# A key's cumulative gate row read from DRAM instead of multiplied out by a selector, and narrow gate weights loaded in an earlier stage

## The chip, the cores and the metric

The kernel runs on one core of one Trainium2 chip. The metric is the device time of one execution in microseconds (us), lower is better. One execution of the program was also recorded by the hardware profiler; rows below come from that record. The engines are named as in the profile: PE is TensorE (matmul), PEld its weight loads, DVE is VectorE, ACT is ScalarE, POOL is GpSimd and SP is SyncE, which here only issues DMAs.

## The reference

The program computes two layers of a decoder on 256 tokens of width 2048. Layer 0 mixes tokens by gated linear attention, layer 1 by "forgetting attention" (FoX, 16 heads of 128); each mixer is followed by a gated MLP with a short convolution (inner width 5632). All is modulated by a conditioning vector `c` through `w_mod`. The change touches the FoX mixer:

```python
def fox_mixer(h, w_in, b_f, q_gain, k_gain, w_out):
    proj = h @ w_in
    q, k, v, og, fl = jnp.split(proj, [D_MODEL, 2 * D_MODEL, 3 * D_MODEL, 4 * D_MODEL], axis=-1)
    ...
    log_f = jax.nn.log_sigmoid((fl + b_f).astype(jnp.float32))
    cum = jnp.cumsum(log_f, axis=1).transpose(0, 2, 1)
    ...
        logits = (jnp.einsum('bhqd,bhkd->bhqk', qb, k).astype(jnp.float32)
                  + cb[..., None] - cum[:, :, None, :])
        logits = jnp.where(key_pos[None, :] <= q_pos[:, None], logits, -jnp.inf)
        p = jax.nn.softmax(logits, axis=-1)
```

`fl` has one column per head (16 columns at the end of `w_in`, the "gate weights"). `cum` is the running sum of the log gates over the tokens. A logit of query i and key j gets `cum[i]` added, which is one number per query, and `cum[j]` subtracted, which is one number per key.

## The kernel before

**Streams.** All large products run in the same way. A weight tile of 128 x 1024 (512 KB) is loaded by SP into a ring of eight buffers (`sync_load`, L259 to L264; `load_to`, L727). ACT casts it into a high part `wh` (L140) and DVE subtracts to get the low part `wl` (L144), both in `split_w`. A product takes three matmuls: high by high, high by low, low by high. `plan` lists all weight tiles in the order of use. `next_w` (L699) hands out the tile of one step, splits up to three steps ahead (`AHEAD`; there are four pairs of split buffers), and loads six further (`LOOK`). Loads of the modulation weights `wm` share the ring and SP's queue.

**Steps.** One step k takes one weight tile against one slice of 128 inputs. `stream_a` (matmul at L779, 24 of 256 columns per step) puts tokens on the free side; `stream_b` (matmul at L860, 12 of 512 columns per step) puts tokens on the partitions. After each step `tick` runs small tasks from the list `side` (as many as `pace["side"]`, about one per step) and background sums of the modulation weights on DVE (L291).

**Order.** The kernel's text gives a program order, and a scheduler that simulates times puts each engine's instructions in a fixed order. Each engine then runs its own list strictly in that order, and waits on semaphores. `issue_after` asks the scheduler to place one instruction behind another. SP's list holds the DMA issues, which stop when the next buffer of the ring isn't free.

**The entry to FoX.** `fox` (L1189) first streams V in two halves of 16 steps. With the first half goes the gate projection, `gate_part`, called once a step as `extra`. From step `GATE_AT` = 9 on, it runs three matmuls a step (L1231) with the gate weights, thirty of them at step 9 for the steps before. The gate weights are one entry of the plan, placed behind step 9's tile: 2048 rows of 16 numbers (64 bytes a row), 128 KB in all, through SP and a ring buffer, split like the others into a tile `nw` of 128 x 368. Then come the log sigmoid and, as a side task, `cums`: transposes to token order (`ltok`), running sums through a triangular matrix `tri`, once per token (`cumt`, the query's number) and once as rows by head (`pn`). The rows are negated and split into a high part (partitions 0 to 15) and a low part (32 to 47) of `nhl`.

**The attention.** Q and K are streamed in four groups; behind each pair `attend(g)` puts the tasks of eight heads on `side`. For head i these are `soft` (scores and softmax), two heads later `turn` (transposes of the weights), three heads later `apply` (product with V). So the first heads of a group follow each other by one or two tasks, later ones by three. In `soft`, the key's row comes onto the scores by a matmul: `sel`, one column of `identr` repeated over 128 columns, picks the two rows of the head out of `nhl` and writes their sum to all 128 partitions in PSUM (L1292, 48 rows by 384 columns), and the score matmuls (L1293, L1294) add to it. DVE adds the query's number while it copies PSUM to the tile `s` (L1296, L1298), POOL masks it (L1301), DVE and ACT form the softmax (L1304 to L1312). There are four buffers for `s` (`SB`).

**Queues.** Loads of weights go through SP. ACT's own queue takes a few small loads at the start and half of the output at the end.

Of the kernel before, what the change touches and what calls it, by code (L numbers as in the profile page):

```python
# [9 lines left out]
F32 = mybir.dt.float32  # L10
# [59 lines left out]
NBIG = 12  # L70
FILL = (0, 7)
FIRST_ORDER = (0, 2, 1)
GATE_AT = 9
TURNS = (0, 2, 1, 3, 4, 6, 5, 7)

HELD = (16, 48)
# [4 lines left out]
def kernel(  # L81
# [46 lines left out]

    def split_w(src, moving, after=None):
        n_ = src.shape[-1]  # L130
        if n_ < 512 and not moving and n_ > 256:
            st = big.tile([P, 2, 512], F32R, tag="s8", name=nm("nw"))
            hi, lo = st[:, 0, :n_], st[:, 1, :n_]
        else:
            hi, lo = split_pair(n_, moving)
        with ExitStack() as es:
            if order["f"] is not None:
                es.enter_context(tc.issue_after(order["f"]))
                order["f"] = None
            order["b"], order["c"] = order["c"], nc.scalar.copy(out=hi, in_=src).ins  # L140
        with ExitStack() as es:
            if after is not None:
                es.enter_context(tc.issue_after(after))
            order["v"] = nc.vector.tensor_tensor(out=lo, in0=src, in1=hi.bitcast(F32), op=ALU.subtract).ins  # L144
        return hi, lo
# [5 lines left out]
    ident = const.tile([P, P], F32, name="ident")  # L151
    make_identity(nc, ident)

    H2 = 2 * FH + 16
    identr = const.tile([H2, FH], F32R, name="identr")
    nc.vector.tensor_tensor(out=identr, in0=ident[:H2, :FH], in1=ident[:H2, 32:32 + FH], op=ALU.add)
    ones = const.tile([P, P], F32, name="ones")
    nc.vector.memset(ones, 1.0)
    one = ones[:, 0:1]
# [1026 lines left out]
        add_residual(l, "g_m", ALL, rhs)  # L1186


    def fox(l, h):  # L1189
# [3 lines left out]
        nhl = tmp.tile([H2, 3 * P], F32R, tag="k1", bufs=1, name="nhl")  # L1193
        ltok = tmp.tile([P, 2, H2], F32, tag="ltok", bufs=1, name="ltok")

        def cums():
            pl = misc()
            for tt in range(TT):
                nc.tensor.transpose(pl[:, tt * FH:(tt + 1) * FH], lf[:, tt * P:(tt + 1) * P], ident[:FH, :FH])
            nc.vector.memset(ltok, 0.0)  # L1200
            for c0 in (0, 32):
                nc.vector.tensor_copy(out=ltok[:, :, c0:c0 + FH], in_=pl[:, :2 * FH].rearrange("p (a b) -> p a b", a=2))
            pc = misc()
            nc.tensor.matmul(pc[:, 0:FH], tri, ltok[:, 0, :FH], start=True, stop=True)
            nc.tensor.matmul(pc[:, FH:2 * FH], ones, ltok[:, 0, :FH], start=True, stop=False)
            nc.tensor.matmul(pc[:, FH:2 * FH], tri, ltok[:, 1, :FH], start=False, stop=True)
            nc.vector.tensor_copy(out=cumt, in_=pc[:, :2 * FH].rearrange("p (a b) -> p a b", a=2))
            pn = misc()
            nc.tensor.matmul(pn[:H2, 0:P], ltok[:, 0, :], tri, start=True, stop=True)
            nc.tensor.matmul(pn[:H2, P:T], ltok[:, 0, :], ones, start=True, stop=False)  # L1210
            nc.tensor.matmul(pn[:H2, P:T], ltok[:, 1, :], tri, start=False, stop=True)
            for cs, src in ((slice(0, P), pn[:H2, 0:P]), (slice(P, 3 * P), pn[:H2, 0:T])):
                nc.scalar.activation(nhl[:, cs], src, AF.Copy, scale=-1.0)
                lo = nhl[32:H2, cs]
                nc.vector.scalar_tensor_tensor(out=lo, in0=src[32:H2], scalar=-1.0, in1=lo.bitcast(F32),
                                               op0=ALU.mult, op1=ALU.subtract)

        pace["side"], pace["sacc"] = 1.0, 0.0
        vt = [bigt([P, D], "v") for _ in range(TT)]
        gates = {}  # L1220

        def gate_part(k):
            if k < GATE_AT:
                return
            if k == GATE_AT:
                gates["w"], gates["p"] = next_w(0, [(4 * D, FH)]), misc()
            for kk in range(0 if k == GATE_AT else k, k + 1):
                gh, gl = h(kk)
                cs = slice(kk * FH, kk * FH + P)
                for i, (w_, r_) in enumerate(((gates["w"][0], gh), (gates["w"][0], gl), (gates["w"][1], gh))):  # L1230
                    nc.tensor.matmul(gates["p"][:, :T], w_[:, cs], r_, start=(kk == 0 and i == 0),  # L1231
                                     stop=(kk == KT - 1 and i == 2), skip_group_check=True)
# [49 lines left out]
                side.append(fin(hp))  # L1282

        pts = {}

        def soft(hd):
            def f():
                q_ = qT[hd // 8][:, hd % 8, :]
                k_ = kT[hd // 8][:, hd % 8, :]
                sel = identr[:, hd:hd + 1].to_broadcast([H2, P])  # L1290
                p_ = misc()
                nc.tensor.matmul(p_[:, 0:3 * P], sel, nhl, start=True, stop=False, skip_group_check=True)  # L1292
                nc.tensor.matmul(p_[:, 0:P], q_[:, 0:P], k_[:, 0:P], start=False, stop=False, skip_group_check=True)  # L1293
                nc.tensor.matmul(p_[:, P:3 * P], q_[:, P:T], k_, start=False, stop=True, skip_group_check=True)  # L1294
# [3 lines left out]
                nc.vector.tensor_scalar(out=s[:, P:3 * P], in0=p_[:, P:3 * P], scalar1=cumt[:, 1, hd:hd + 1],  # L1298
                                        scalar2=None, op0=ALU.add)
# [301 lines left out]
    def between():  # L1601
# [1 line left out]
        queue(mod_tasks(0, "g_f"))  # L1603
        queue_halves(1, "m")
        pace["bg"] = SLOW
    ffn(0, lazy(make_h(0, "f"), KT, 2, (8,)), (ALL[:8], between, lambda: set_pace(N2)))
    drain_bg()

    queue(mod_tasks(1, "g_m"))
# [59 lines left out]
```

## Time and profile before

| | us |
|---|---|
| median of three runs | 2412.05 |
| lowest and highest of the three | 2410.41 and 2412.06 |
| the profiled execution, its own time | 2411.13 |
| its span, first to last instruction | 2409.4 |

| engine | busy us | share of the span |
|---|---|---|
| PE | 2369.6 | 98% |
| PEld | 2274.7 | 94% |
| DVE | 1886.2 | 78% |
| ACT | 1347.1 | 56% |
| POOL | 45.6 | 2% |

The mean granted clock of PE was 0.996. DMA moved 638.31 MB, a mean of 265 GB/s.

How to read it: the span is cut by engine, and engines run side by side, so busy times add up to more than the span. A matmul's busy time reaches from its start to its last result, and the next one starts before that; the distance of two starts tells what a matmul costs in a full stream. "Idle before" is the time an engine stood ahead of an instruction, with what ended it. The chain of waits follows the path back from the last instruction.

### The profile page before, as it was taken

The numbers are of one execution on the slowest core, as the hardware profiler recorded it, in microseconds if no ns is written. First come the engines' busy times: TensorE is split into PE (matmuls) and PEld (weight loads), VectorE is DVE, ScalarE is ACT, GpSimd is POOL, SyncE is SP. The second block draws the span as 40 slices with busy tenths as digits, with TensorE's granted clock in tenths as the row PEclk, the third lists the DMA queues.
The fourth block names the chain that finished last, engine by engine and source line by source line (L and its number), as shares of the span: only waits on it lengthen the run. The fifth ranks groups of instructions, "written<-read, shape, count | busy, mean of one in ns | idle before, by whom it ended". The sixth has DMA issues, their size and how long they took to land.

```text
span 2409.4 us, 46946 instructions
## 1 busy us (share of the span) xinstructions
PE 2369.6 (98%) x19028; PEld 2274.7 (94%) x19030; DVE 1886.2 (78%) x2478; ACT 1347.1 (56%) x1932; POOL 45.6 (2%) x93
## 2 busy tenths in 40 slices
PE   7999999999999999999999999999999999999998
PEld 5899889999999999999888879999999999999998
DVE  5787979887679999986678888888777777777544
ACT  4668764645776566443554455545755555565433
POOL 0000000000000000000000201100000000000000
PEclk9999999999999999999999999999999999999999
DMA  9898869797669988998589877786777777766552
GB/s 375 326 353 297 312 229 325 275 361 273 199 200 310 314 310 311 324 315 301 158 297 314 303 267 236 241 296 234 227 236 237 228 235 236 235 206 216 192 191 101
DMA packets 188293, 638.31 MB, mean 265 GB/s; under 512 B 23849, under 2 KB 24859, under 8 KB 187692
## 3 DMA queue, kind: packets, MB, share of 16 engines
q1 hardware_dynamic: 187112, 634.12, 77.0%
q8 instruction: 149, 2.44, 0.4%
q10 hardware_dynamic: 964, 1.20, 0.1%
q14 instruction: 68, 0.56, 0.1%
HBM read 633.14 MB, written 2.10 MB: 264 GB/s over the span
## 4 chain that ended last, share of the span: by engine, by line
PE 92%; DVE 3%; DMA 3%; ACT 1%; issue 1%; DVEq 0%; SPq 0%; ACTq 0%
PE pa L779 74%; PE pa L860 14%; DMA wm<-in_w_mod_dram 1%; DVE wl L144 1%; DMA w<-in_fox_w_in_dram 0%; DVE acc L291 0%; DMA w<-in_gla_w_in_dram 0%; DVE hn L623 0%; PE pm L1103 0%; PE pm L1330 0%; PE pm L1276 0%; PE pm L1294 0%; ACT wh L140 0%; PE pm L1293 0%; PE pm L1125 0%
## 5 line engine op out<-in xcount | busy, mean ns | idle before, releaser
L140 ACT CAST wh<-w 128x1024 fp32r<-128x1024 f32 x816 | 852.1, 1049 | 903.2 <-PE pa L779 651.4
L144 DVE TENSOR_TENSOR wl<-w,wh 128x1024 fp32r<-128x1024 f32 x816 | 991.7, 1218 | 405.4 <-ACT wh L140 399.3
L779 PE MATMUL pa<-h,wh 128*128 128x256 f32 x7168 | 1223.5, 278 | 5.0 <-DVE h L653 3.6
L779 PEld LDWEIGHTS pa<-h,wh 128*128 128x128 f32 x7168 | 1073.9, 188 | 10.5 <-DVE h L653 4.2
L779 PE MATMUL pa<-h,wl 128*128 128x256 f32 x3584 | 966.3, 277 | 1.9 <-DVE wl L144 1.9
L779 PEld LDWEIGHTS pa<-h,wl 128*128 128x128 f32 x3584 | 662.5, 188 | 2.7 <-DVE wl L144 2.5
L779 PE MATMUL pa<-op,wh 128*128 128x256 f32 x3840 | 651.6, 277 | 0.4 <-DVE op L683 0.2
L779 PEld LDWEIGHTS pa<-op,wh 128*128 128x128 f32 x3840 | 573.0, 188 | 1.4 <-DVE xT L912 1.0
L779 PE MATMUL pa<-op,wl 128*128 128x256 f32 x1920 | 518.0, 276 | 0.0
L291 DVE SCALAR_TENSOR_TENSOR acc<-wm,cT,acc 128x1024 f32<-128x1024 f32 (+2 forms) x360 | 444.4, 1235 | 15.1 <-DMA wm<-in_w_mod_dram 13.9
L779 PEld LDWEIGHTS pa<-op,wl 128*128 128x128 f32 x1920 | 355.0, 188 | 0.0
L860 PE MATMUL pa<-wh,h 128*128 128x512 f32 x1024 | 312.0, 394 | 0.2 <-ACT h L644 0.2
L860 PEld LDWEIGHTS pa<-wh,h 128*128 128x128 f32 x1024 | 191.1, 188 | 40.3 <-ACT h L644 0.9
L860 PE MATMUL pa<-wl,h 128*128 128x512 f32 x512 | 191.8, 394 | 0.0
L860 PEld LDWEIGHTS pa<-wl,h 128*128 128x128 f32 x512 | 96.5, 189 | 19.5
L1382 ACT ACTIVATE y<-u,cw 128x256 f32<-128x256 f32 x176 | 101.7, 599 | 3.3 <-DVE act L1398 1.3
L1385 DVE SCALAR_TENSOR_TENSOR y<-u,cw,y 128x254 f32<-128x254 f32 x176 | 83.3, 479 | 2.9
L1383 DVE SCALAR_TENSOR_TENSOR y<-u,cw,y 128x255 f32<-128x255 f32 x176 | 84.0, 477 | 0.0
L1404 ACT COPY u<-pa 128x512 f32<-128x512 f32 x112 | 63.6, 582 | 2.1 <-PE pa L779 1.2
L644 ACT ACTIVATE h<-hn,mod 128x256 fp32r<-128x256 f32 x58 | 32.4, 596 | 14.0 <-DVE hn L623 11.3
L1392 ACT ACTIVATE u<-y 128x256 f32<-128x256 f32 x88 | 36.0, 413 | 3.3 <-DVE y L1385 3.1
L1398 DVE TENSOR_TENSOR act<-u,y 128x256 f32<-128x256 f32 x88 | 36.7, 420 | 1.4
(274 smaller groups left out, 1044.5 us busy)
## 6 DMA issues: line engine op xcount, KB each, us to landing
wm<-in_w_mod_dram SPq DMA_DIRECT2D x320, 512.0 KB, 5.3
w<-in_ffn_w_up_dram SPq DMA_DIRECT2D x320, 512.0 KB, 4.5
w<-in_ffn_w_down_dram SPq DMA_DIRECT2D x176, 512.0 KB, 4.6
w<-in_fox_w_in_dram SPq DMA_DIRECT2D x128, 512.0 KB, 5.2
w<-in_gla_w_in_dram SPq DMA_DIRECT2D x96, 512.0 KB, 7.1
w<-in_gla_w_out_dram SPq DMA_DIRECT2D x32, 512.0 KB, 5.9
w<-in_ffn_w_up_dram SPq DMA_DIRECT2D x64, 256.0 KB, 4.0
w<-in_fox_w_out_dram SPq DMA_DIRECT2D x32, 512.0 KB, 5.1
```

Of the source, the lines that this page charges most:

```text
L140: order["b"], order["c"] = order["c"], nc.scalar.copy(out=hi, in_=src).ins
L144: order["v"] = nc.vector.tensor_tensor(out=lo, in0=src, in1=hi.bitcast(F32), op=ALU.subtract).ins
L291: nc.vector.scalar_tensor_tensor(out=st["a"], in0=wt[:, j, :], scalar=col, in1=st["a"], op0=ALU.mult, op1=ALU.add)
L644: hot = nc.scalar.activation(hi, t, AF.Identity, scale=sc, bias=sh).ins
L779: mm = nc.tensor.matmul(o, w_[:, ms], r_, start=(first and i == 0 and m % 2 == 0), stop=last and i == 2, skip_group_check=True)
L860: mm = nc.tensor.matmul(o, l_[:, ts_], w_[:, hs_], start=first and i == 0, stop=last and i == 2, skip_group_check=True)
L1382: nc.scalar.activation(y, u, AF.Identity, scale=cw[:, l * 3 + 2, r:r + 1], bias=cw[:, 6 + l, r:r + 1])
L1383: nc.vector.scalar_tensor_tensor(out=y[:, 1:], in0=u[:, :T - 1], scalar=cw[:, l * 3 + 1, r:r + 1], in1=y[:, 1:], op0=ALU.mult, op1=ALU.add)
L1385: nc.vector.scalar_tensor_tensor(out=y[:, 2:], in0=u[:, :T - 2], scalar=cw[:, l * 3, r:r + 1], in1=y[:, 2:], op0=ALU.mult, op1=ALU.add)
L1392: nc.scalar.activation(u, y, AF.Silu)
L1398: nc.vector.tensor_tensor(out=act[m // 8][:, m % 8, :], in0=sg, in1=y, op=ALU.mult)
L1404: nc.scalar.copy(out=u[:, 2 * b:2 * b + 2, :], in_=ps[b])
```

## The change

**The gate weights.** They leave the plan. A new function `load_gate` clears the tail of a tile of 128 x 368 on POOL and loads the 128 KB from ACT's queue. It is called from `settle`, which the first MLP runs at the start of the seventh of its up-projection's column groups. `gate_part` now makes the cast (ACT) and the subtraction (DVE) itself at step `GATE_AT` - 2 = 5 of the first V half, placed behind the last weight cast and subtraction issued by then. The gate matmuls start at step 7 (24 at once, then three a step).

**The key's row.** `nhl`, `identr` and the selector matmul go. `cums` copies the rows `pn` to SBUF on ACT and stores them with SP into a DRAM tensor `crows` of 16 x 256. `key_row(hd)` takes a buffer of `s` and loads row `hd`, repeated over 128 partitions, into its columns 128 to 383, through SP. It is called at the start of `soft` for the next head, and for the first head of a group as a side task of its own. In `soft` the first score matmul starts the sum, and the two DVE instructions become `scalar_tensor_tensor`: score plus the query's number minus the row, the second of them in place.

**Beside it.** `ltok` is 16 columns per token block and not 48 and needs no clearing. A small unused tile `spare` is set to zero at the start. The branch of `split_w` for the gate weights goes.

```diff
-GATE_AT = 9
+GATE_AT = 7
...
+    dram = ctx.enter_context(tc.tile_pool(name="dram", bufs=1, space=bass.MemoryType.DRAM))
...
-    identr = const.tile([H2, FH], F32R, name="identr")
-    nc.vector.tensor_tensor(out=identr, in0=ident[:H2, :FH], in1=ident[:H2, 32:32 + FH], op=ALU.add)
+    spare = const.tile([48, FH], F32, name="spare")
+    nc.vector.memset(spare, 0.0)
...
+    def load_gate():
+        raw_gate["w"] = w_ = tmp.tile([P, GW], F32, tag="k1", bufs=1, name="rg")
+        nc.gpsimd.memset(w_[:, KT * FH:], 0.0)
+        nc.scalar.dma_start(out=w_[:, :KT * FH].rearrange("p (k r) -> p k r", r=FH),
+                            in_=fox_w_in[0, :, 4 * D:4 * D + FH].rearrange("(k p) r -> p k r", p=P))
...
-            nc.vector.memset(ltok, 0.0)
-            for c0 in (0, 32):
-                nc.vector.tensor_copy(out=ltok[:, :, c0:c0 + FH], in_=pl[:, :2 * FH].rearrange("p (a b) -> p a b", a=2))
+            nc.vector.tensor_copy(out=ltok, in_=pl[:, :2 * FH].rearrange("p (a b) -> p a b", a=2))
...
-            for cs, src in ((slice(0, P), pn[:H2, 0:P]), (slice(P, 3 * P), pn[:H2, 0:T])):
-                nc.scalar.activation(nhl[:, cs], src, AF.Copy, scale=-1.0)
-                lo = nhl[32:H2, cs]
-                nc.vector.scalar_tensor_tensor(out=lo, in0=src[32:H2], scalar=-1.0, in1=lo.bitcast(F32),
-                                               op0=ALU.mult, op1=ALU.subtract)
+            crow_ = t1("cr")[:FH, :]
+            nc.scalar.copy(out=crow_, in_=pn[:FH, :T])
+            nc.sync.dma_start(out=crows, in_=crow_)
...
         def gate_part(k):
+            if k == GATE_AT - 2:
+                with ExitStack() as es:
+                    es.enter_context(tc.issue_after(order["c"]))
+                    es.enter_context(tc.issue_after(order["v"]))
+                    st = big.tile([P, 2, 512], F32R, tag="s8", name=nm("nw"))
+                    gates["w"] = st[:, 0, :GW], st[:, 1, :GW]
+                    nc.scalar.copy(out=gates["w"][0], in_=raw_gate["w"])
+                    nc.vector.tensor_tensor(out=gates["w"][1], in0=raw_gate["w"], in1=gates["w"][0].bitcast(F32),
+                                            op=ALU.subtract)
             if k < GATE_AT:
                 return
             if k == GATE_AT:
-                gates["w"], gates["p"] = next_w(0, [(4 * D, FH)]), misc()
+                gates["p"] = misc()
...
+        def key_row(hd):
+            s = rows_of[hd] = tmp.tile([P, 3 * P], F32, tag="s", bufs=SB, name=nm("s"))
+            nc.sync.dma_start(out=s[:, P:3 * P], in_=crows[hd:hd + 1, :].to_broadcast([P, T]))
 
         def soft(hd):
             def f():
+                if hd % 8 < 7:
+                    key_row(hd + 1)
...
-                sel = identr[:, hd:hd + 1].to_broadcast([H2, P])
                 p_ = misc()
-                nc.tensor.matmul(p_[:, 0:3 * P], sel, nhl, start=True, stop=False, skip_group_check=True)
-                nc.tensor.matmul(p_[:, 0:P], q_[:, 0:P], k_[:, 0:P], start=False, stop=False, skip_group_check=True)
+                nc.tensor.matmul(p_[:, 0:P], q_[:, 0:P], k_[:, 0:P], start=True, stop=True, skip_group_check=True)
                 nc.tensor.matmul(p_[:, P:3 * P], q_[:, P:T], k_, start=False, stop=True, skip_group_check=True)
-                s = tmp.tile([P, 3 * P], F32, tag="s", bufs=SB, name=nm("s"))
-                nc.vector.tensor_scalar(out=s[:, 0:P], in0=p_[:, 0:P], scalar1=cumt[:, 0, hd:hd + 1],
-                                        scalar2=None, op0=ALU.add)
-                nc.vector.tensor_scalar(out=s[:, P:3 * P], in0=p_[:, P:3 * P], scalar1=cumt[:, 1, hd:hd + 1],
-                                        scalar2=None, op0=ALU.add)
+                s = rows_of.pop(hd)
+                nc.vector.scalar_tensor_tensor(out=s[:, 0:P], in0=p_[:, 0:P], scalar=cumt[:, 0, hd:hd + 1],
+                                               in1=s[:, P:2 * P], op0=ALU.add, op1=ALU.subtract)
+                nc.vector.scalar_tensor_tensor(out=s[:, P:3 * P], in0=p_[:, P:3 * P], scalar=cumt[:, 1, hd:hd + 1],
+                                               in1=s[:, P:3 * P], op0=ALU.add, op1=ALU.subtract)
...
         def attend(g):
             h0 = g * 8
+            side.append(lambda: key_row(h0))
...
-    plan_stream(fox_w_in[0], ALL[:GATE_AT + 1], [(2 * D, 1024)], True)
-    plan.append((fox_w_in[0], 0, KT, ((4 * D, FH),), False))
-    plan_stream(fox_w_in[0], ALL[GATE_AT + 1:], [(2 * D, 1024)], True)
-    for c0 in (2 * D + 1024, 0, D, 1024, D + 1024, 3 * D, 3 * D + 1024):
+    for c0 in (2 * D, 2 * D + 1024, 0, D, 1024, D + 1024, 3 * D, 3 * D + 1024):
         plan_stream(fox_w_in[0], ALL, [(c0, 1024)], c0 < 3 * D)
...
+    def settle():
+        set_pace(N2)
+        load_gate()
+    ffn(0, lazy(make_h(0, "f"), KT, 2, (8,)), (ALL[:8], between, settle))
```

More of the change, by code (lines that the diff above doesn't have):

```diff
@@ L130, in split_w @@
         n_ = src.shape[-1]
[L131 to L135, printed above, removed]
+        hi, lo = split_pair(n_, moving)
         with ExitStack() as es:
@@ L1186, in gla_rest @@
         add_residual(l, "g_m", ALL, rhs)
+    GW = KT * FH + P - FH
+    raw_gate = {}
+    def load_gate():
[3 more added lines that the diff above has]
+                            in_=fox_w_in[0, :, 4 * D:4 * D + FH].rearrange("(k p) r -> p k r", p=P))
     def fox(l, h):
@@ L1192, in fox @@
         cumt = tmp.tile([P, 2, FH], F32, tag="cumt", bufs=1, name="cumt")
-        nhl = tmp.tile([H2, 3 * P], F32R, tag="k1", bufs=1, name="nhl")
-        ltok = tmp.tile([P, 2, H2], F32, tag="ltok", bufs=1, name="ltok")
+        ltok = tmp.tile([P, 2, 48], F32, tag="ltok", bufs=1, name="ltok")[:, :, :FH]
+        crows = dram.tile([FH, T], F32, name="crows")
         def cums():
@@ L1199, in cums @@
                 nc.tensor.transpose(pl[:, tt * FH:(tt + 1) * FH], lf[:, tt * P:(tt + 1) * P], ident[:FH, :FH])
-            nc.vector.memset(ltok, 0.0)
-            for c0 in (0, 32):
-                nc.vector.tensor_copy(out=ltok[:, :, c0:c0 + FH], in_=pl[:, :2 * FH].rearrange("p (a b) -> p a b", a=2))
+            nc.vector.tensor_copy(out=ltok, in_=pl[:, :2 * FH].rearrange("p (a b) -> p a b", a=2))
             pc = misc()
-            nc.tensor.matmul(pc[:, 0:FH], tri, ltok[:, 0, :FH], start=True, stop=True)
-            nc.tensor.matmul(pc[:, FH:2 * FH], ones, ltok[:, 0, :FH], start=True, stop=False)
-            nc.tensor.matmul(pc[:, FH:2 * FH], tri, ltok[:, 1, :FH], start=False, stop=True)
+            nc.tensor.matmul(pc[:, 0:FH], tri, ltok[:, 0, :], start=True, stop=True)
+            nc.tensor.matmul(pc[:, FH:2 * FH], ones, ltok[:, 0, :], start=True, stop=False)
+            nc.tensor.matmul(pc[:, FH:2 * FH], tri, ltok[:, 1, :], start=False, stop=True)
             nc.vector.tensor_copy(out=cumt, in_=pc[:, :2 * FH].rearrange("p (a b) -> p a b", a=2))
             pn = misc()
-            nc.tensor.matmul(pn[:H2, 0:P], ltok[:, 0, :], tri, start=True, stop=True)
-            nc.tensor.matmul(pn[:H2, P:T], ltok[:, 0, :], ones, start=True, stop=False)
-            nc.tensor.matmul(pn[:H2, P:T], ltok[:, 1, :], tri, start=False, stop=True)
-            for cs, src in ((slice(0, P), pn[:H2, 0:P]), (slice(P, 3 * P), pn[:H2, 0:T])):
-                nc.scalar.activation(nhl[:, cs], src, AF.Copy, scale=-1.0)
-                lo = nhl[32:H2, cs]
-                nc.vector.scalar_tensor_tensor(out=lo, in0=src[32:H2], scalar=-1.0, in1=lo.bitcast(F32),
-                                               op0=ALU.mult, op1=ALU.subtract)
+            nc.tensor.matmul(pn[:FH, 0:P], ltok[:, 0, :], tri, start=True, stop=True)
+            nc.tensor.matmul(pn[:FH, P:T], ltok[:, 0, :], ones, start=True, stop=False)
+            nc.tensor.matmul(pn[:FH, P:T], ltok[:, 1, :], tri, start=False, stop=True)
+            crow_ = t1("cr")[:FH, :]
+            nc.scalar.copy(out=crow_, in_=pn[:FH, :T])
+            nc.sync.dma_start(out=crows, in_=crow_)
         pace["side"], pace["sacc"] = 1.0, 0.0
@@ L1284, in fox @@
         pts = {}
+        rows_of = {}
+        def key_row(hd):
+            s = rows_of[hd] = tmp.tile([P, 3 * P], F32, tag="s", bufs=SB, name=nm("s"))
+            nc.sync.dma_start(out=s[:, P:3 * P], in_=crows[hd:hd + 1, :].to_broadcast([P, T]))
         def soft(hd):
             def f():
+                if hd % 8 < 7:
+                    key_row(hd + 1)
                 q_ = qT[hd // 8][:, hd % 8, :]
                 k_ = kT[hd // 8][:, hd % 8, :]
[L1290 removed]
                 p_ = misc()
[L1292 to L1293 removed]
+                nc.tensor.matmul(p_[:, 0:P], q_[:, 0:P], k_[:, 0:P], start=True, stop=True, skip_group_check=True)
                 nc.tensor.matmul(p_[:, P:3 * P], q_[:, P:T], k_, start=False, stop=True, skip_group_check=True)
[L1295 to L1299 removed]
+                s = rows_of.pop(hd)
[3 more added lines that the diff above has]
+                                               in1=s[:, P:3 * P], op0=ALU.add, op1=ALU.subtract)
                 dv = s.rearrange("p (j t) -> p j t", j=3)[:, 0:3:2, :]
@@ L1605, in between @@
         pace["bg"] = SLOW
-    ffn(0, lazy(make_h(0, "f"), KT, 2, (8,)), (ALL[:8], between, lambda: set_pace(N2)))
+    def settle():
+        set_pace(N2)
+        load_gate()
+    ffn(0, lazy(make_h(0, "f"), KT, 2, (8,)), (ALL[:8], between, settle))
     drain_bg()
```

1 line of the change is left out of this document (removed).

## The prediction

> **What bounds the kernel now.** First the page: busy shares and the chain that ended last.
>
> ```profile
> span 2409.4 us, 46946 instructions
> PE 2369.6 (98%) x19028; PEld 2274.7 (94%) x19030; DVE 1886.2 (78%) x2478; ACT 1347.1 (56%) x1932; POOL 45.6 (2%) x93
> PE 92%; DVE 3%; DMA 3%; ACT 1%; issue 1%; DVEq 0%; SPq 0%; ACTq 0%
> ```
>
> TensorE holds the path nearly everywhere. So an edit pays in two ways only: it takes matmul time away, or it takes away a place where PE stands still. Two stretches matter: the entry to the fox layer, and the attention. First the chain at the entry.
>
> ```profile
> 1187.90 10.89 DMA w<-in_fox_w_in_dram
> 1198.82 0.51 ACT nw L140
> 1199.37 0.80 PE pm L1231 x2
> ```
>
> The narrow gate weights (2048 rows of 64 bytes) are issued at 1187.90 and land 10.89 us later; ACT casts them, and only then can PE go on. The timeline shows the price on PE (start, length, engine, line; in brackets the idle time before it).
>
> ```profile
> 1187.90 0.38 SPq L264 DMA_DIRECT2D w<-in_fox_w_in_dram  x1
> ...
> 1199.37 0.80 PE L1231 MATMUL pm<-h,nw 128*128 128x256 f32 x2 [2.53 <-ACT nw L140]
> 1199.96 0.63 PE L860 MATMUL pa<-wh,h 128*128 128x512 f32 x1
> 1200.39 0.63 PE L860 MATMUL pa<-wl,h 128*128 128x512 f32 x1
> ...
> 1202.47 0.39 PE L860 MATMUL pa<-wh,h 128*128 128x512 f32 x1
> 1202.70 0.40 PE L860 MATMUL pa<-wl,h 128*128 128x512 f32 x1
> ```
>
> ```profile
> 1199.00:1202.40 3.40, 3.04 (x8) 2.55 (x9) 2.62 (x5) 3.40 (x6) 0.00 (x0) 0.50 0.76 251
> ```
>
> The last row is a stretch (width; PE, PEld, DVE, ACT and POOL busy; clock; DMA share; GB/s). PE stands for 2.53 us, and comes back with a granted clock of 0.50: a 512-column matmul starts every 0.43 us there (1199.96 to 1200.39) and every 0.23 us from 1202.47 on.
>
> In the attention the same view, over the 190 us in which all sixteen heads lie, and the waits there:
>
> ```profile
> 1380.00:1570.00 190.00, 189.52 (x1224) 167.88 (x1224) 163.95 (x305) 100.03 (x175) 25.54 (x48) 1.00 0.76 254
> ```
>
> ```profile
> ACT wh L140 <- PE pa L860: 27.3, 17, 3.0
> ACT wh L140 <- PE pa L779: 19.6, 13, 3.2
> ```
>
> PE is full (189.52 of 190), and ACT, which casts the next weights, waits for PE to give buffers back: the weights run ahead. VectorE has 26 us free. The path here is PE's instructions.
>
> **The gate weights, loaded early.** The stall goes if the weights lie in SBUF long before. It costs 2.53 us of standing, and then the slow clock: from 1199.37 to 1202.47 are 3.10 us, in which two 256-column and six 512-column matmuls ran; at full clock these are 2 x 0.115 + 6 x 0.23 = 1.6 us, so 1.5 us are lost. Together **4.0 us**. The 48 gate matmuls stay; they only start two k-steps sooner.
>
> What is late next? The cast and subtraction of the gate weights now come behind the weight splits of step k = 5. Their lengths, and the room there:
>
> ```profile
> L140 ACT CAST nw<-w x1: 497/497/497, 1198.8 to 1198.8; 128x368 fp32r<-128x368 f32 x1
> L144 DVE TENSOR_TENSOR nw<-w,nw x1: 543/543/543, 1199.3 to 1199.3; 128x368 fp32r<-128x368 f32 x1
> ```
>
> ```profile
> 1190.00:1195.00 5.00, 5.00 (x24) 4.12 (x23) 3.54 (x8) 2.21 (x4) 0.00 (x0) 1.00 0.55 92
> ```
>
> ACT has 2.8 and DVE 1.5 us free in these 5 us, before PE needs the result, so 0.5 and 0.54 us fit: zero; if the cover were gone, about 0.5 us. Behind the gate cast ACT had the next weight cast queued; freed of that wait, it runs ahead. One ring buffer and 2048 small descriptors leave SP's queue, so the weights behind them come sooner.
>
> The load itself moves to ACT's queue at the seventh column group of the first up-projection. By the loops, five groups of 16 steps and 88 steps of the down-projection lie between that and the fox layer: 168 steps of 24 matmuls (24 x 0.115 = 2.76 us each, by the spacing shown below), 464 us, so it falls near 1188 - 464, about 720 us. It costs ACT an issue (0.38 us on SP above), and its descriptors share the DMA engines with the weight loads:
>
> ```profile
> 725.00:730.00 5.00, 5.00 (x47) 5.00 (x46) 5.00 (x8) 2.27 (x4) 0.00 (x0) 1.00 0.89 288
> w<-in_ffn_w_up_dram SPq DMA_DIRECT2D x320, 512.0 KB, 4.5
> ```
>
> A weight load is issued six steps, about 16.5 us, before its cast, and takes 4.5 us. Were it held for the whole 10.89 us it would take 15.4 us, still in time: zero, at most a repeat of the 4.0 us there. The Trainium skill speaks against hoping for more: "DMA: Bandwidth & Descriptors", section "Issuing engines are not separate DMA queues", says that DMAs of all issuing engines share the same 16 DMA engines and interleave, another issuer saving only issue time. By that rule the 10.89 us are moved, not removed, and the gain rests on the lead alone; no run here shows this load on ACT's queue yet.
>
> **The selector matmuls, taken out.** One head on PE, and an apply step just before it, which has no such matmul:
>
> ```profile
> 1560.82 0.28 PE L779 MATMUL pa<-h,wl 128*128 128x256 f32 x1
> 1560.94 0.59 PE L1330 MATMUL pm<-pt,v 128*128 128x256 f32 x2
> 1561.37 0.38 PE L1331 MATMUL pm<-pt,v 128*128 128x128 f32 x2
> 1561.51 0.48 PE L779 MATMUL pa<-h,wh 128*128 128x256 f32 x2
> 1561.83 0.28 PE L779 MATMUL pa<-h,wl 128*128 128x256 f32 x1
> ...
> 1562.31 0.39 PE L779 MATMUL pa<-h,wh 128*128 128x256 f32 x2
> 1562.63 0.43 PE L1292 MATMUL pm<-nhl,identr 48*128 48x384 f32 x1
> 1562.99 0.49 PE L1293 MATMUL pm<-kT,qT 128*128 128x128 f32 x2
> 1563.32 0.60 PE L1294 MATMUL pm<-kT,qT 128*128 128x256 f32 x2
> 1563.57 0.47 PE L779 MATMUL pa<-h,wl 128*128 128x256 f32 x1
> 1563.87 0.40 PE L779 MATMUL pa<-h,wh 128*128 128x256 f32 x2
> ```
>
> ```profile
> L1292 PE MATMUL pm<-nhl,identr x16: 435/438/443, 1400.7 to 1562.6; 48*128 48x384 f32 x16
> ```
>
> Lengths overlap, so starts count. A 256-column matmul of L779 starts every 0.115 us; after the two at 1562.31 the next was due at 1562.54. L1292 begins at 1562.63, L1293 at 1562.99: 0.45 us for 384 columns. By columns alone it would be 1.5 x 0.115 = 0.17 us; the rest is standing on either side. That is the lower bound: 16 x 0.17 = 2.7 us, if the standing stays with the fp32 matmuls behind. The upper one: the whole head takes 1562.54 to 1563.76 (1563.87 less one spacing), 1.22 us; the apply with as many columns as L1293 and L1294 (768) takes 1560.94 to 1561.60, 0.66 us; the difference 0.56 us gives 9.0 us. I take 0.45, since L1330, fp32 as well, is entered without a gap (0.12 us after L779): the gap belongs to the 48-row matmul. 16 x 0.45 = **7.2 us**.
>
> The Trainium skill, "TensorEngine Tiling (Array Packing)", section "Key Properties", says that a change of tiling mode drains TensorE. Whether 48 rows are such a change no row here proves; the gaps agree. By the rule the standing goes with the selector and the sum is 16 x 0.45; without it, 16 x 0.17.
>
> On VectorE the two adds from PSUM get a second tensor operand:
>
> ```profile
> L1298 DVE TENSOR_SCALAR s<-pm,cumt x16: 465/474/476, 1403.5 to 1564.6; 128x256 f32<-128x256 f32 x16
> L912 DVE SCALAR_TENSOR_TENSOR xT<-pa,mod,xT x64: 469/476/485, 402.0 to 2397.5; 128x256 f32<-128x256 f32 x64
> ```
>
> 476 against 474 ns for the same size from PSUM: zero. Making the hi and lo rows (two ACT, two DVE instructions) gives way to one ACT copy and a store; PE's matmuls there stay in number, and the store has some 150 us before the first head. Zero; the setup's memset for an add too.
>
> New are sixteen row loads on SP (one a head, 128 pieces of 1 KB) and a wait of VectorE for each. A row is asked for one head ahead. Bounds for its landing:
>
> ```profile
> w<-in_fox_w_in_dram SPq DMA_DIRECT2D x128, 512.0 KB, 5.2
> wg<-in_gla_w_gate_dram SPq DMA_DIRECT2D x1, 64.0 KB, 2.0
> ```
>
> 2.0 to 5.2 us. Heads mostly stand three side tasks apart, three k-steps or over 8 us, so the row is there. In each group the first three follow at one step (2.76 us), and there VectorE may wait up to some 3 us, six times, with the next weight subtraction queued behind it and PE behind that. Splits run up to three steps (8 us) ahead and VectorE has 26 us free, so I count zero for the end. On SP a row load waits until the transposes of four heads before have given back its score buffer (four of them); behind it stand weight loads with a lead of six steps.
>
> **Sum:** 4.0 + 7.2 = 11.2 us. The profiled execution took 2411.13 us (span 2409.4 and 1.7 around it), 0.9 under the median of 2412.05; so 2399.9 for such an execution and **2400.9** for the median.
>
> **Rivals.** (1) The standing around the selector stays with the fp32 matmuls: 2.7 + 4.0 = 6.7 us, 2405.4. For it: PE queue gaps lie also before L1293. Against: L1330. (2) The stall at the fox entry is only exchanged, for a late weight around 720 us or a gate cast that comes late: only 7.2 us, 2404.9. Against: the lead. (3) Both, or half the gain lost to small waits in a new order of instructions: 2.7 to 5.6 us, 2406.5 to 2409.4. (4) **Slower: the rows land late and VectorE becomes the bound.** Place: the head's first subtraction, VectorE in order, weight subtractions queued behind. With w us per head the stage takes 163.95 + 16 w on VectorE; it passes the old 190 us at w = 1.6, and the gate's 4.0 us are used up at w = 1.9. At w = 2.6, half a landing, the stage is 15.6 us longer, less 4.0: 2423.7; with the whole 5.2 us, 2465. For it: SP is in order behind weight loads that wait for ring buffers. Against: the lead of a head.
>
> **How the numbers follow.** Forecast 0.56 (2399 to 2403); rival 1 0.10; rival 2 0.10; rival 3 0.13; rival 4 0.11. About 0.2% (4.8 us) is what a measurement of this kernel can tell from no change, so faster means below 2407.2. Faster: 0.56 + 0.10 + 0.10 and a small part of rival 3, 0.78; the same 0.11; slower 0.11. The range starts at the upper bound of the selector (9.0 + 4.0 = 13.0, 2399.0, less 1 for the spread of runs) and reaches over rivals 1 to 3 to 2409; rival 4 stays out.
>
> **What would show it.** In the changed kernel's timeline no idle PE before the first L1231-like matmul and a clock of 1.00 around it; between 1375 and 1570 no 48-row matmul, and L1293's successor starting 0.12 us after the projection matmul ahead of it; ACT still waiting for PE in that stage. The forecast is wrong if VectorE shows waits for a DMA of the row tensor over 2 us a head, if PE waits for a weight subtraction in the attention, or if a new PE stall stands near 720 us.

## The result, and the profile after

| | before | after |
|---|---|---|
| median of the timed runs, us | 2411.23 | 2396.85 |
| lowest to highest, us (four runs each) | 2409.45 to 2412.06 | 2394.97 to 2400.05 |
| profiled execution, us (its span) | 2411.13 (2409.4) | 2400.05 (2398.3) |

The ratio is 0.9944 with a 95% interval of 0.9932 to 0.9956: 14.4 us less by the medians. The sign of the forecast came true, and so did its two causes (shown in the experiments below); the size was forecast as 11.2 us, and the time lies 1.15 us under the lower end of the range, 2398 us.

The page of the changed kernel, its busy times and the engines of the chain that ended last:

```profile
span 2398.3 us, 46949 instructions
PE 2361.9 (98%) x19012; PEld 2272.7 (95%) x19014; DVE 1886.0 (79%) x2473; ACT 1347.4 (56%) x1931; POOL 47.2 (2%) x94
PE 91%; DMA 3%; DVE 3%; ACT 2%; issue 1%; SPq 0%; DVEq 0%; ACTq 0%
```

It is still PE's kernel. PE has 16 matmuls less (the selectors) and 7.7 us less of busy time; DVE and ACT are as before. (PE's rows are counted as the trace holds them: it lists two matmul records for one instruction on fp32 operands, such as the score matmuls. Line numbers move by the edit: the projection matmuls L779 and L860 are now L775 and L856, the scores L1293 and L1294 are L1308 and L1309, the gate's L1231 is L1241.)

The two profiled executions differ by only 11.1 us in their spans. To see the change alone, a stage is cut out that begins and ends with the same matmul: the token sum after the first mixer and the one after the second. First before, then after (median lengths in ns, then the first and the last start in us):

```profile
L522 PE MATMUL pm<-sq,onesD x12: 379/379/415, 446.8 to 1672.3; 128*128 128x256 f32 x12
```

```profile
L518 PE MATMUL pm<-sq,onesD x12: 379/379/414, 449.5 to 1661.3; 128*128 128x256 f32 x12
```

The stage took 1225.5 us and takes 1211.8: **13.7 us less**. Ahead of it, this one execution of the changed kernel was 2.7 us later than before's; in the other traces below, the second one of the changed kernel among them (447.3), that point lies between 443.9 and 447.5 us, so this is spread of the first 450 us and not the change. The stage is the ruler for all that follows: the six traces of the changed kernel and of those variants whose edit leaves the stage alone or only moves the gate weights' load or use give 1211.6 to 1211.8 us.

The entry to the FoX layer after, in the timeline: the cast and subtraction of the gate weights, the first gate matmuls, and a stretch around them (width; PE, PEld, DVE, ACT, POOL busy; clock; DMA share; GB/s).

```profile
1195.40 0.49 ACT L1230 CAST nw<-rg 128x368 fp32r<-128x368 f32 x1
...
1197.42 0.54 DVE L1231 TENSOR_TENSOR nw<-rg,nw 128x368 fp32r<-128x368 f32 x1
...
1199.53 0.40 PE L1241 MATMUL pm<-h,nw 128*128 128x256 f32 x2
```

```profile
1196.00:1200.00 4.00, 4.00 (x21) 3.33 (x20) 3.94 (x7) 4.00 (x8) 0.00 (x0) 1.00 0.84 225
```

No bracket stands behind the gate matmuls: PE comes to them without a pause, 4.00 us busy of 4.00 and at a clock of 1.00, where before it stood for 2.53 us and came back at 0.50.

One head of the attention on PE after, to be laid beside the one in the prediction:

```profile
1556.58 0.28 PE L775 MATMUL pa<-h,wl 128*128 128x256 f32 x1
1556.70 0.38 PE L1308 MATMUL pm<-kT,qT 128*128 128x128 f32 x2
1556.92 0.60 PE L1309 MATMUL pm<-kT,qT 128*128 128x256 f32 x2
1557.16 0.59 PE L775 MATMUL pa<-h,wh 128*128 128x256 f32 x2
1557.59 0.28 PE L775 MATMUL pa<-h,wl 128*128 128x256 f32 x1
```

The head is due at 1556.70 and the stream is back in step at 1557.59 less two spacings of 0.115, 1557.36: 0.66 us, against 1.22 before. That is 0.56 us a head less, the upper bound of the prediction and not the 0.45 it took. Where the other 0.11 lay, the lengths of the first score matmuls show, before and after:

```profile
L1293 PE MATMUL pm<-kT,qT x32: 275/326/377, 1401.0 to 1563.2; 128*128 128x128 f32 x32
```

```profile
L1308 PE MATMUL pm<-kT,qT x32: 270/273/275, 1399.2 to 1556.8; 128*128 128x128 f32 x32
```

One of each pair took up to 377 ns behind the selector; all take 273 now. The start of the second score step came 0.33 us after the first (1562.99 to 1563.32), and comes 0.22 us after it now. The selector's cost ran on into the matmul behind it.

The stage of the attention, and the row tensor:

```profile
1375.00:1570.00 195.00, 195.00 (x1319) 179.19 (x1318) 175.55 (x318) 107.30 (x186) 29.86 (x51) 1.00 0.83 278
```

```profile
L1299 SPq DMA_DIRECT2D s<-crows x16: 326/327/789, 1247.4 to 1543.6; - x16
DMA to landing us min/median/max: 3.1/5.8/6.7
```

PE is busy for all of 195 us (before it stood for 0.48 us at 1534). No wait of DVE for a row shows among the waits, though a row takes 5.8 us to land (the prediction had 2.0 to 5.2). The first four loads (there are four buffers of `s`) were issued from 1247.4 on, some 150 us before the first head, and not where the text calls them. The shortest lead of the sixteen is that of the last head: its row is asked for at 1543.60 and first read by DVE at 1557.55, 13.9 us later, twice the longest landing.

### The profile page after: what moved, and what is told of

It is laid out like the page before. It is cut to its first block, busy times and chain, and to the rows that moved or that the text cites. A ratio compares the mean times of both kernels' runs of the same rounds, so it can differ in the third digit from the quotient of the medians.

```text
span 2398.3 us, 46949 instructions
## 1 busy us (share of the span) xinstructions
PE 2361.9 (98%) x19012; PEld 2272.7 (95%) x19014; DVE 1886.0 (79%) x2473; ACT 1347.4 (56%) x1931; POOL 47.2 (2%) x94
## 4 chain that ended last, share of the span: by engine, by line
PE 91%; DMA 3%; DVE 3%; ACT 2%; issue 1%; SPq 0%; DVEq 0%; ACTq 0%
PE pa L775 74%; PE pa L856 13%; DMA w<-in_gla_w_in_dram 1%; DMA wm<-in_w_mod_dram 1%; DVE wl L141 1%; ACT wh L137 0%; PE pm L1099 0%; PE pm L1286 0%; PE pm L1309 0%; PE pm L1345 0%; DVE acc L287 0%; DVE hn L619 0%; PE pm L1121 0%; PE pm L1241 0%; DMA xtok<-in_x_dram 0%
## 5 line engine op out<-in xcount | busy, mean ns | idle before, releaser
L775 PE MATMUL pa<-h,wh 128*128 128x256 f32 x7168 | 1226.3, 278 | 5.1 <-DVE h L649 3.6
L775 PEld LDWEIGHTS pa<-h,wh 128*128 128x128 f32 x7168 | 1075.9, 189 | 10.5 <-DVE h L649 4.2
L775 PE MATMUL pa<-h,wl 128*128 128x256 f32 x3584 | 967.7, 278 | 2.1 <-DVE wl L141 2.1
L775 PEld LDWEIGHTS pa<-h,wl 128*128 128x128 f32 x3584 | 663.7, 189 | 3.1 <-DVE wl L141 2.9
L775 PE MATMUL pa<-op,wh 128*128 128x256 f32 x3840 | 652.2, 277 | 0.4 <-DVE op L679 0.2
L775 PEld LDWEIGHTS pa<-op,wh 128*128 128x128 f32 x3840 | 572.9, 188 | 1.4 <-DVE xT L908 1.0
L775 PE MATMUL pa<-op,wl 128*128 128x256 f32 x1920 | 517.9, 276 | 0.6 <-DVE wl L141 0.6
L775 PEld LDWEIGHTS pa<-op,wl 128*128 128x128 f32 x1920 | 355.1, 188 | 0.8 <-DVE wl L141 0.8
L856 PE MATMUL pa<-wh,h 128*128 128x512 f32 x1024 | 311.0, 394 | 0.6 <-ACT pa L757 0.4
L856 PEld LDWEIGHTS pa<-wh,h 128*128 128x128 f32 x1024 | 190.3, 188 | 41.2 <-ACT h L640 0.9
L856 PE MATMUL pa<-wl,h 128*128 128x512 f32 x512 | 189.8, 393 | 0.1
L856 PEld LDWEIGHTS pa<-wl,h 128*128 128x128 f32 x512 | 95.9, 188 | 20.1 <-DVE wl L141 0.5
L640 ACT ACTIVATE h<-hn,mod 128x256 fp32r<-128x256 f32 x58 | 32.4, 596 | 14.4 <-DVE hn L619 11.7
```

Of the source, the lines that this page charges most:

```text
L640: hot = nc.scalar.activation(hi, t, AF.Identity, scale=sc, bias=sh).ins
L775: mm = nc.tensor.matmul(o, w_[:, ms], r_, start=(first and i == 0 and m % 2 == 0), stop=last and i == 2, skip_group_check=True)
L856: mm = nc.tensor.matmul(o, l_[:, ts_], w_[:, hs_], start=first and i == 0, stop=last and i == 2, skip_group_check=True)
```

## The experiments

Times set beside each other were taken side by side on the same chip. "The stage" is the one cut out above.

**1. The gate weights alone.** The kernel before with the new `load_gate`, `settle` and `gate_part` and the plan without the gate entry; `nhl`, `identr` and the selector are kept (`nhl` takes its buffer in `cums`, since the raw gate weights hold it until then).

```diff
-GATE_AT = 9
+GATE_AT = 7
...
+    def load_gate():
...
+            if k == GATE_AT - 2:
...
         def cums():
+            nhl = nhls["t"] = tmp.tile([H2, 3 * P], F32R, tag="k1", bufs=1, name="nhl")
```

> The gate weights loaded early, the selector matmuls kept. Theory: the stall at the fox entry (2.53 us) and the slow clock behind it (1.5 us) go and nothing takes their place: 4.0 us less than the kernel before. Rival: the stall is exchanged for one elsewhere (late weights where the load now lies): no difference, 0 to 1 us.

Measured: 2406.51 us against 2411.39; ratio 0.9982 (0.9973 to 0.9990), 4.3 us by the ratio.

```profile
L522 PE MATMUL pm<-sq,onesD x12: 379/379/417, 446.5 to 1667.7; 128*128 128x256 f32 x12
```

The stage takes 1221.2 us, 4.3 less than before. The 4.0 us of the prediction hold, and PE has no wait in this trace between 1185 and 1215 us: nothing took the stall's place there.

**2. The rows alone.** The changed kernel with the gate weights back in the plan.

```diff
-GATE_AT = 7
+GATE_AT = 9
...
-    for c0 in (2 * D, 2 * D + 1024, 0, D, 1024, D + 1024, 3 * D, 3 * D + 1024):
+    plan_stream(fox_w_in[0], ALL[:GATE_AT + 1], [(2 * D, 1024)], True)
+    plan.append((fox_w_in[0], 0, KT, ((4 * D, FH),), False))
...
```

> The key's rows from DRAM, the gate weights through the plan as before. Theory, as the traces of before and after now read: a head is 1.22 us shorter by 0.56 on TensorE, 16 x 0.56 = 9.0 us, and the 0.48 us of standing at 1534 go with it: 9.5 us less than before. The prediction's size was 7.2 us; by columns alone 2.7 us.

Measured: 2401.72 us against 2411.39; ratio 0.9960 (0.9948 to 0.9972).

```profile
L522 PE MATMUL pm<-sq,onesD x12: 379/379/416, 447.5 to 1663.4; 128*128 128x256 f32 x12
```

The stage takes 1215.9 us, 9.6 less: 16 x 0.56 = 9.0 and the 0.48 us of standing. The stage shows no wait of PE between 1375 and 1570 us. The parts add up: 4.3 + 9.6 = 13.9, the whole change 13.7.

**3. The selector on 112 rows.** Does the cost belong to the selector's height? The kernel before, with zeros in 64 further rows. (All 128 rows don't fit: the pool `tmp` would need 27.84 KB a partition, and 27.78 KB are left, so there is no time for that height.)

```diff
-    H2 = 2 * FH + 16
+    H2 = 112
...
-                lo = nhl[32:H2, cs]
+                lo = nhl[32:48, cs]
...
-                nc.vector.scalar_tensor_tensor(out=lo, in0=src[32:H2], scalar=-1.0, in1=lo.bitcast(F32),
+                nc.vector.scalar_tensor_tensor(out=lo, in0=src[32:48], scalar=-1.0, in1=lo.bitcast(F32),
```

> The kernel before with the selector on 112 rows and not 48 (the 64 rows more are zeros); same columns, same repeated weight column, same places. If the standing belongs to the 48-row height: a head shrinks from 1.22 us to 0.17 for the columns + 0.66, so 16 x 0.39 = 6.2 us less than before, and L1293 starts 0.17 us after the selector. If it belongs to the repeated weight column or to the change from fp32r to fp32: no difference.

Measured: 2404.48 us against 2410.29; ratio 0.9978 (0.9967 to 0.9988). A head in its timeline, and the stage:

```profile
1557.45 0.34 PE L1292 MATMUL pm<-nhl,identr 112*128 112x384 f32 x1
1557.63 0.38 PE L1293 MATMUL pm<-kT,qT 128*128 128x128 f32 x2
1557.85 0.60 PE L1294 MATMUL pm<-kT,qT 128*128 128x256 f32 x2
1558.10 0.47 PE L779 MATMUL pa<-h,wl 128*128 128x256 f32 x1
1558.40 0.40 PE L779 MATMUL pa<-h,wh 128*128 128x256 f32 x2
```

```profile
L522 PE MATMUL pm<-sq,onesD x12: 379/379/411, 447.2 to 1666.8; 128*128 128x256 f32 x12
```

With more than twice the rows the same matmul costs 0.18 us (1557.45 to 1557.63), which is its columns, and the score matmul behind it has its 0.22 us. The head, from 1557.45 to 1558.40 less one spacing, takes 0.83 us, against 1.22 before: 0.39 us less, as expected. The stage takes 1219.6 us, 5.9 less than before. The repeated weight column and the change from fp32r to fp32 are still there, so they weren't this cost. So the 9.6 us of experiment 2 are 2.7 for the selector's columns, 5.9 for its height and 0.5 for the standing at 1534, which is still 0.5 us here; 0.5 us are left unplaced.

**4. The selector behind the scores.** The kernel before, with the selector matmul as the last of its head.

```diff
-                nc.tensor.matmul(p_[:, 0:3 * P], sel, nhl, start=True, stop=False, skip_group_check=True)
-                nc.tensor.matmul(p_[:, 0:P], q_[:, 0:P], k_[:, 0:P], start=False, stop=False, skip_group_check=True)
-                nc.tensor.matmul(p_[:, P:3 * P], q_[:, P:T], k_, start=False, stop=True, skip_group_check=True)
+                nc.tensor.matmul(p_[:, 0:P], q_[:, 0:P], k_[:, 0:P], start=True, stop=False, skip_group_check=True)
+                nc.tensor.matmul(p_[:, P:3 * P], q_[:, P:T], k_, start=False, stop=False, skip_group_check=True)
+                nc.tensor.matmul(p_[:, 0:3 * P], sel, nhl, start=False, stop=True, skip_group_check=True)
```

> The kernel before with the selector matmul behind the two score matmuls of its head, 48 rows as before. If the standing belongs to the 48-row matmul it moves with it: the first score matmul starts 0.12 us after the projection matmul ahead of it, and gaps stand on both sides of the selector; the head takes 1.1 to 1.2 us, the time is within 0.1% of before. If it belongs to the change from fp32r to fp32, the first score matmul keeps a gap and the selector loses it.

Measured: 2410.59 us against 2410.29; ratio 1.0004 (0.9995 to 1.0013); the stage takes 1225.6 us (443.9 to 1669.5), as before. A head:

```profile
1559.82 0.28 PE L779 MATMUL pa<-h,wh 128*128 128x256 f32 x1
1559.94 0.38 PE L1292 MATMUL pm<-kT,qT 128*128 128x128 f32 x2
1560.16 0.60 PE L1293 MATMUL pm<-kT,qT 128*128 128x256 f32 x2
1560.68 0.44 PE L1294 MATMUL pm<-nhl,identr 48*128 48x384 f32 x1
1561.05 0.39 PE L779 MATMUL pa<-h,wh 128*128 128x256 f32 x1
1561.28 0.28 PE L779 MATMUL pa<-h,wl 128*128 128x256 f32 x1
```

The first score matmul, fp32 behind fp32r, now starts 0.12 us after the projection matmul, with no gap. The gaps have moved with the 48-row matmul: the step ahead of it takes 0.52 us (0.24 in the changed kernel), and the matmul behind it 0.23 us where 0.115 is the spacing.

**5. The rows late.** To price the fourth rival: the row of a head is asked for only when its scores lie in PSUM.

```diff
-                if hd % 8 < 7:
-                    key_row(hd + 1)
...
+            nc.scalar.copy(out=s[:, P:P + 1], in_=p_[:, P:P + 1])
             nc.sync.dma_start(out=s[:, P:3 * P], in_=crows[hd:hd + 1, :].to_broadcast([P, T]))
...
+                key_row(hd, p_)
                 s = rows_of.pop(hd)
...
-            side.append(lambda: key_row(h0))
```

> The changed kernel, but a head's row is asked for only when its scores lie in PSUM (ACT copies one score into the row's buffer first, which the load then overwrites), so each head waits a whole landing, about 5.7 us, on VectorE, and SP waits for the scores before it goes on. Rival 4's sum (VectorE becomes the bound: 163.95 + 16 x 5.7 = 255 us against a stage of 181): over 60 us slower than the changed kernel. If the scheduler puts other work before each waiting instruction and splits run ahead: 0 to 15 us slower.

Measured: 2412.42 us against 2411.61 before and 2397.72 for the changed kernel beside it: 14.7 us more than the changed kernel. The profiled execution is the longest of the eleven (2415.77); its stage takes 1230.0 us (447.0 to 1677.0). Among its waits (us in total, times, longest), and a stretch:

```profile
DVE s L1311 <- DMA s<-crows: 22.0, 10, 3.8
PE pm L1307 <- DVE s L1313: 2.6, 2, 1.4
PE pm L1345 <- DVE s L1313: 2.5, 1, 2.5
PE pm L1336 <- DVE s L1325: 2.1, 1, 2.1
```

```profile
1375.00:1595.00 220.00, 209.94 (x1385) 191.59 (x1384) 179.66 (x325) 113.31 (x211) 29.47 (x49) 0.96 0.76 254
```

DVE waits ten times, 22 us in all, and not sixteen times 5.7. PE stands for 10.1 us of the 220 where it stood for none, and runs at a mean clock of 0.96: 10 us and about 0.04 x 210 = 8 us, the 18.2 us by which the stage is longer than the changed kernel's. All of PE's standing lies before matmuls of the heads themselves (scores, transposes, product with V), mostly until DVE has worked on a head's late scores; none of it ends with a weight subtraction or a weight load. So the danger was real, at a quarter of the 60 us named first and inside the 0 to 15 us named second, but not by the path of rival 4: VectorE did not become the bound (179.66 us busy and 22 waiting of 220). Why six heads found their row in time was not followed line by line. By the medians, asking late costs 14.7 us, more than the selector's removal gained.

**6. Where the gate load lies.** In the changed kernel the load was not issued near 720 us:

```profile
L1191 ACTq DMA_DIRECT2D rg<-in_fox_w_in_dram x1: 403/403/403, 236.7 to 236.7; - x1
```

The scheduler drew it forward to 236.7 us, right behind the last use of the buffer's former tile. Two kernels bind it in ACT's order, at the place where the text calls it and at the entry to the FoX layer (the last two pieces of the edit are in the second kernel alone).

```diff
+        with tc.issue_after(order["c"]):
             nc.scalar.dma_start(out=w_[:, :KT * FH].rearrange("p (k r) -> p k r", r=FH),
...
     def fox(l, h):
+        load_gate()
...
         set_pace(N2)
-        load_gate()
```

> The changed kernel with the gate load bound behind the weight cast issued when the seventh column group starts, so that it is issued near 720 us, as the prediction had it, and not at 236.7 us, where the scheduler put it. If the load costs the GLA stage time: up to 1 us less than the changed kernel (2396.85 us), and the stage from 219.8 to 255 us as long as before. If not: the same within 0.1%. A new stall near 720 us: 1 to 4 us more.

> The changed kernel with the gate load on ACT's queue, but bound behind the last weight cast ahead of the fox layer (about 1172 us). If the gain needs the early load: the 10.9 us of landing end near 1183 to 1187, ahead of the cast at step 5 (near 1193 us), so no loss, 0 to 0.5 us; then it was SP's order and the late issue that cost, not the load's length. If its pieces crowd out the weights at the entry: 1 to 4 us slower than the changed kernel.

Measured: 2396.70 us against 2411.39 for the first and 2396.97 against 2411.61 for the second; the stages take 1211.6 and 1211.7 us. In the first the load is issued at 710.3 us, and nothing changes in the first layer: from the last L900 to the last L1018 (the gate of layer 0) it takes 33.2 us there, 33.1 in the second profile of the changed kernel. In the second:

```profile
L1192 ACTq DMA_DIRECT2D rg<-in_fox_w_in_dram x1: 403/403/403, 1163.2 to 1163.2; - x1
L1232 ACT CAST nw<-rg x1: 501/501/501, 1192.3 to 1192.3; 128x368 fp32r<-128x368 f32 x1
```

A lead of 29 us does as well as one of 959 us (236.7 to 1195.4). A start some 25 us sooner than the old 1187.90, on ACT's queue, was enough; whether the same start on SP's queue would do was not tried.

**7. Smaller checks.** The changed kernel again:

> The changed kernel once more, for its spread: 11 to 16 us less than before. If the first 450 us of an execution vary by themselves, its trace stands closer to before's there than the 2.7 us of the first trace.

2397.72 us against 2411.61 (ratio 0.9944, 0.9931 to 0.9956), the stage 1211.6 us (447.3 to 1658.9).

The gate matmuls from step 9 again, the cast left at step 5:

```diff
-GATE_AT = 7
+GATE_AT = 9
...
-            if k == GATE_AT - 2:
+            if k == 5:
```

> The changed kernel with the gate matmuls starting at step 9, as before, and not 7; the load and the cast stay early. If only the load's place gave the gain: the same as the changed kernel within 0.1%. If the two steps matter: up to 1 us more.

2397.21 us against 2410.29 (ratio 0.9948, 0.9933 to 0.9964), the stage 1211.6 us: the two steps give nothing.

**8. The same cure elsewhere.** The first layer has four matmul instructions of 17 rows by 512 columns, eight records in the trace, in three places (two, two and four records). With the load near 720 us kept, their operands were widened to 112 rows, the weights' further rows zero.

```diff
-        wg = ringt([P, 1024], "wg")[:RANK + 1, :]
+        wg = ringt([P, 1024], "wg")[:112, :]
+        nc.gpsimd.memset(wg, 0.0)
...
-                    parts[key] = tmp.tile([RANK + 1, 3 * P], F32, tag="k1", bufs=1, name="aT")
+                    parts[key] = tmp.tile([112, 3 * P], F32, tag="k1", bufs=1, name="aT")
```

> The changed kernel with the gate load near 720 us, and with the eight 17-row matmuls of the first layer's gate (log-gate logits, 17 rows by 512 columns) on 112 rows, the rows more of the weights being zeros. They stand in three groups, and around each the start times show standing as around the 48-row selector. If that standing goes and TensorE is the bound there: about 3 x 0.4 = 1.2 us less than the changed kernel. If the chain of ACT's log sigmoid sets the end of that stage, as the chain of waits has it: the same within 0.1%.

Measured: 2397.47 us against 2409.52; ratio 0.9949 (0.9935 to 0.9963). The first pair in the changed kernel (its second profile) and here:

```profile
225.91 0.28 PE L775 MATMUL pa<-h,wh 128*128 128x256 f32 x1
226.12 1.12 PE L999 MATMUL pm<-wg,aT 17*128 17x512 f32 x2
227.17 0.39 PE L775 MATMUL pa<-h,wh 128*128 128x256 f32 x1
227.40 0.28 PE L775 MATMUL pa<-h,wl 128*128 128x256 f32 x1
```

```profile
224.49 0.28 PE L775 MATMUL pa<-h,wh 128*128 128x256 f32 x1
224.61 1.02 PE L1000 MATMUL pm<-wg,aT 112*128 112x512 f32 x2
225.06 0.68 PE L775 MATMUL pa<-h,wh 128*128 128x256 f32 x1
225.58 0.28 PE L775 MATMUL pa<-h,wl 128*128 128x256 f32 x1
```

From the start of the pair to the next matmul the cost falls from 1.05 to 0.45 us, but that cut again leaves out a stretched neighbour: the matmul behind the wide pair takes 0.52 us (225.06 to 225.58), the one behind the narrow pair 0.23. Counted as for a head, from where the place is due (one spacing of 0.115 after the projection matmul ahead) to where the stream is back in step, the pair takes 1.26 us on 17 rows and 0.86 on 112, 0.40 us less. The place with four records in a row takes 2.1 and 1.7 us, also 0.4 less, and a selector 0.39 less (experiment 3). So what the height costs goes by the place, and not by the number of narrow matmuls in it.

PE's work there is thus some 1.2 us shorter, as expected, and the time is the same: the next stage starts at 447.0 us, not sooner than the 446.4 and 447.3 us of its neighbours. The chain of waits of the changed kernel (second profile) says why:

```profile
232.11 1.06 ACT le L941
...
235.42 1.06 ACT le L942
...
243.16 1.07 ACT le L942
...
244.26 1.24 DVE la L943
...
245.54 1.60 PE pm L1018 x12
```

These are ACT's exponential and logarithm of the log sigmoid (`le`), then DVE, and PE waits for them. With the wide operands PE only waits longer, and comes back slower. The changed kernel (second profile), then the wide one:

```profile
245.54 1.60 PE L1018 MATMUL pm<-mgla,la 128*128 128x128 f32 x12 [1.61 <-DVE la L943]
```

```profile
243.53 2.56 PE L1019 MATMUL pm<-mgla,la 128*128 128x128 f32 x12 [2.20 <-DVE la L943]
```

After 1.61 us of standing the granted clock was 1.00, after 2.20 us it was 0.50 from 244 to 247 us, so that the same twelve matmuls took 2.56 us and not 1.60. From the last L900 to the end of the gate this one execution needs 34.2 us, against 33.2 in experiment 6. No kernel tried was measurably faster than the changed one.

## Why the prediction was right or wrong

**What bounds it: right.** Every gain came from PE's time or PE's standing; after the change PE is still full in the attention and ACT waits for it:

```profile
ACT wh L137 <- PE pa L775: 25.7, 18, 3.0
ACT wh L137 <- PE pa L856: 19.9, 13, 2.4
```

**The gate, 4.0 us: right**, 4.3 measured (experiment 1). The reading of the slow clock as part of the stall's price belongs to it: standing alone would have been 2.53 us. The step "about 720 us" was wrong for the kernel as it was scheduled, since the loops of the text don't fix the place of an instruction that waits only for its buffer (bound to its place in experiment 6, the load goes out at 710.3); it cost the forecast nothing, because the stage is the same at the three places tried. The prediction said that the gain rests on the lead alone; a lead of 29 us was enough, and whether the queue plays a part stays open.

**The selector, 7.2 us: the step that failed.** The term was mis-sized, 0.45 us a head where 0.56 was removed: 9.0 us by the heads, 9.6 by the stage. The mechanism, standing that belongs to the 48-row matmul, is shown by experiments 3 and 4, and rival 1 (2.7 us) is out. The size came out small for two reasons. The cut was made at the start of L1293, though the matmul behind the selector was stretched too: 0.11 us a head, 1.8 us in all. The bound from the whole head against the apply step (0.56) had held just that, and should have been taken: it compares a stream with the thing against a stream without it, and needs no line between the two. The other 0.5 us are PE's standing at 1534, a wait of an apply step for DVE, which the prediction did not count. It is there in the traces with the selector (0.5 us in experiments 1 and 3, 0.3 in experiment 4) and gone in those with rows from DRAM asked for early; what in their order of instructions removes it was not followed.

On the rule that was weighed there, the Trainium skill, "TensorEngine Tiling (Array Packing)", section "Key Properties" (a change of tiling mode drains TensorE): the traces agree as far as they go. At 48 rows the 384 columns cost 0.56 us with gaps on both sides, at 112 rows 0.18 us, and the extra goes by the place (experiment 8). No run here shows the mode itself, so that the height is the cost is shown, and that it is such a change is not.

**VectorE's adds, the hi and lo rows, the store: zero, right.** The two adds take 344 and 479 ns (medians) against 346 and 474, and DVE's busy time is 1886.0 us against 1886.2.

**The row loads: zero, right, but for another reason.** The prediction allowed up to 3 us of waiting for the first heads of a group. There was none, because the loads went out 13.9 us or more ahead of their use, and not one head ahead; that this order of the scheduler would come was not foreseen, so this zero owes something to luck. The landing itself was longer than the bounds of 2.0 to 5.2 us: 5.8 in the median, 6.7 at most. Rival 4 names a true danger, which experiment 5 brings about; its price was too high (2465 us by whole landings, 2423.7 by half of one; 2412.42 measured), since it charged the same wait to all sixteen heads, and its path, VectorE as the bound, is not the one seen there.

**The range.** Its lower end was the right upper bound (13.0 us for both terms) and 1 us for the spread of runs. Missing were the 0.5 us at 1534, and the spread: the four runs of the changed kernel lie over 5 us, and those of the kernel before, over all the comparisons, between 2406.55 and 2417.13 us. Of the 4.05 us between the forecast 2400.9 and the measured 2396.85, 2.5 are the size in the stage (13.7 against 11.2), 0.8 the median of the kernel before, which was 2411.23 in the comparison and not 2412.05, and the other 0.7 lie outside the stage, within the spread. So that the time fell 1.15 us below the range is in part chance: the second set of runs of the changed kernel has its median at 2397.72, 0.28 us below.

## What to carry to other kernels

A matmul on few rows inside a stream of full-height ones can cost three times its columns; count from where it was due to where the stream is back in step, since its neighbours are stretched too, and fill its operands up with zero rows before going further. But measure first that PE is what the place waits for: the same cure gave 5.9 us in the attention, and in the first layer the 1.2 us that PE saved went into a longer wait. A small, piecemeal load belongs well ahead of its use (29 us were enough here for a load that had taken 10.9), and the place where it really goes out is read from the trace, not from the text.

## What the runs showed of the hardware that was not expected

A matmul of 384 columns in a stream of 128-row matmuls cost 0.56 us on 48 rows and 0.18 us on 112. Two matmul records of 512 columns took 1.26 us with their surroundings on 17 rows and 0.86 us on 112, four in a row 2.1 and 1.7 us: about 0.4 us a place each time, however many narrow matmuls stand in it. Between 48 and 112 rows nothing was tried, so where it changes stays open; and the 0.86 us are 0.4 more than the columns of the two (2 x 0.23 us), for a reason that no run here separates.

The standing of 2.53 us at the FoX entry was followed by a granted clock of 0.50 for about 3 us; without the standing the clock stayed at 1.00. Standing of 2.20 us (experiment 8), 2.45 and 2.09 us (experiment 5) was followed by 0.50 too, standing of 1.61 us was not. The length alone does not decide: the same wait of 1.96 us, near 331 us, was followed by 0.50 in the second profile of the changed kernel and by 1.00 in that of the kernel before.
